# A two-block transformer kernel: another order of the opening stage, a norm's sum of squares by products with ones, and stores moved to ScalarE and GpSimd

## The chip, the cores and the metric

The kernel runs on one core of a Trainium2 chip. The metric is the device time of one execution in microseconds. The core has TensorE (PE, matrix products; PEld its weight loads), VectorE (DVE), ScalarE (ACT), GpSimd (POOL) and SyncE (SP); each works through its own queue in order, and waits on semaphores for the others and for transfers. SyncE computes nothing: it issues DMA transfers. ScalarE and GpSimd can issue them too, from their own queues, between their other instructions.

## What is computed

Two transformer blocks in a row on one sequence of 512 tokens with 1024 channels: the first with two layers (modulation from a condition vector, pooling, neighbourhood attention, retention, a convolutional feed-forward part), the second with latent attention, a long convolution (Hyena), attention to a memory of 256 tokens and a mixture of experts. Three pieces matter here, since they do not depend on the first block's result and are computed at the very start: the convolution filters, keys and values of the memory, and the first layer's modulation.

```python
def _hyena_filters(L, w1, b1, freq, w2, b2, w3, b3, decay):
    ...
    h = jnp.sin(fr[0] * (z @ w1.astype(f32) + b1.astype(f32)))
    h = jnp.sin(fr[1] * (h @ w2.astype(f32) + b2.astype(f32)))
    h = h @ w3.astype(f32) + b3.astype(f32)
    h = h * jnp.exp(-t01[:, None] * jnp.abs(decay.astype(f32))[None, :])
    ...
    return jnp.fft.rfft(k, axis=0)

def _mem_xattn(hx, hm, w_mq, w_mkv, w_mo):
    ...
    k, v = jnp.split(hm @ w_mkv, 2, axis=-1)
    ...

# in second_block, hm is _rms(mem, mem_norm_g[l]); in first_block:
mx = jnp.split(silu_c @ w_mod[l] + b_mod[l], 6, axis=-1)
```

## The kernel before

Activations lie with channels on the 128 partitions and tokens along the free dimension. A product of full precision is made of three (`mm3`, lines 198 to 200): each operand is split into a high part in the fast format and a low part, and high x high, low x high and high x low are summed in one bank of PSUM. A weight of 128x1024 is loaded by SyncE, its high part is cast by ScalarE (L181) and its low part subtracted by VectorE (L182). Products whose operands are plain f32 (L296, L309, L407, L1142, L1168) show up in the trace as two instructions each.

The opening is `first` (line 1666). It has five generators, each of which yields after a piece of work, and a written-out order of letters, `START` (line 53), and a shorter one, `SECOND`, say which generator goes on next. A framework below then puts the instructions of each engine in their final order, by its own estimate of when their inputs are ready; so the letters set priorities, and the order shown further down is what each engine's queue really holds.

- `f`: the filters (`hyena_filters`, line 1122). Small tables are loaded, two small products (L1142) each feed a sine: five VectorE operations bring the argument into range, ScalarE takes the sine (L1144 to L1120). Then, for each of two filter sets, eight products with `hy_w3` (L1168) whose results VectorE and ScalarE window and split, and a Fourier transform by products with tables (`transform`, L198 to L200 with `hs0h` and so on, 512 columns). Each transform pair is copied (`hodd`, L1193), added and subtracted by VectorE (L1194, L1195) into `ho`, which has one buffer, and stored to `kf_dram` (L1196); a row of alternating sums goes to `kx_dram`.
- `m`: the memory (`memory`, line 1436). Squares by ScalarE (L319, L322), their running sum by GpSimd (L323); a product with ones turns the sum over channels into a column per token (L296), a root and a reciprocal of a few columns follow, a product spreads it over the partitions again (L309), VectorE multiplies (L335) and each chunk is split into `mmh` (L343, ScalarE) and `mml` (L344, VectorE). Then eight key columns of 24 products each (256 wide), copied by ScalarE (L1450) and stored to `mk_dram`, and the values, 96 products of 512 columns in four PSUM banks, copied into `mvo`, which has one buffer, and stored to `mv_dram`.
- `d`: modulation (`modulation`, line 397). Sixteen weight tiles of 512 KB through two buffers, `mraw`, each used by two products of two rows (L407). These occupy a 32-column quarter of TensorE each. The other two thirds of the layer's modulation use the same code later, in the background.
- `h`: the eight loads of the stream. `n`: the norm of the tokens, behind which layer 0's first products (`lin<-ah`) wait.

Of the kernel before, what the change touches and what calls it, by code (L numbers as in the profile page):

```python
# [11 lines left out]
F32 = mybir.dt.float32  # L12
FR = mybir.dt.float32r
I32 = mybir.dt.int32
AF = mybir.ActivationFunctionType
ALU = mybir.AluOpType
AX = mybir.AxisListType

P = 128
D = 1024  # L20
KC = D // P
S = 512
C = 256
# [26 lines left out]
CONV = "a a a * b a b * * a a a b * a b a * b c c b b b * c b c * d d c c * c d * c d c d d d d d + +".split()  # L50


START = "m f m m m f f f m m f m f m m h h h h h h d f h f d d d d h f d d f d f d d m m m f d m n f f f d d n m m d d n m m d d n m n".split()
SECOND = "f n n n n f f n f n n f n".split()
TILES = 48

# [49 lines left out]
class Builder:  # L106
# [1015 lines left out]
    def hyena_filters(self):  # L1122

        nc, a = self.nc, self.a
        self.kf = self.tc.dram_tile([2, 2, P, 4, S], F32, name="kf_dram")
        self.kx = self.tc.dram_tile([2, 1, 3, S], F32, name="kx_dram")
        small = self.t([64, 6], F32, "hyv", 1)  # L1130
        nc.sync.dma_start(small, a["hyv"])
        zt = self.t([33, S], F32, "hz", 1)
        nc.sync.dma_start(zt, a["hyz"])
        w12 = self.t([64, 128], F32, "hw", 1)
        nc.sync.dma_start(w12[:33, :64], a["hy_w1"])
        nc.sync.dma_start(w12[:, 64:], a["hy_w2"])
        tcol = self.t([P, 16], F32, "htc", 1)
        nc.sync.dma_start(tcol, a["hytc"])
        x = zt
        for i in range(2):  # L1140
            ps = self.psum("pt")[:64, :]
            nc.tensor.matmul(ps, w12[:33 if i == 0 else 64, 64 * i:64 * i + 64], x, start=True, stop=True)  # L1142
            arg = self.t([P, S], F32, "he0", 1)[:64]
            nc.vector.tensor_scalar(out=arg, in0=ps, scalar1=small[:, 2 * i:2 * i + 1],  # L1144
                                    scalar2=small[:, 2 * i + 1:2 * i + 2], op0=ALU.add, op1=ALU.mult)
            y = self.t([65, S], F32, f"hh{i}", 1)
            self.sin(y[:64], arg)
            x = y[:64]
            yield
        nc.gpsimd.memset(y[64:65], 1.0)  # L1150
        skip = self.t([1, 2 * S], F32, "hskip", 1)
        nc.sync.dma_start(skip, a["hy_skip"])
        alt = self.t([P, 8], FR, "halt", 1)
        nc.vector.tensor_copy(alt, tcol[:, 8:16])
        for n in range(2):
            n0 = slice(1024 * n, 1024 * n + 1024)
            w3 = self.t([65, 1024], F32, "hw3", 1)
            nc.sync.dma_start(w3, a["hy_w3b"][:, n0])
            dec = self.t([P, 1024], F32, "hdec", 1)
            nc.sync.dma_start(dec, a["hy_decay"][:, n0].broadcast_to([P, 1024]))  # L1160
            nc.scalar.activation(out=dec, in_=dec, func=AF.Abs)
            both = [[[self.t([P, S], FR, f"hs{sd}" + x, 4) for _ in range(4)] for x in "hl"] for sd in range(2)]
            for tcn in range(4):
                h = []
                for d in range(2):
                    c = slice(512 * d, 512 * d + 512)
                    ps = self.psum("pt")
                    nc.tensor.matmul(ps, y[:, tcn * P:tcn * P + P], w3[:, c], start=True, stop=True)  # L1168
                    e = self.t([P, S], F32, f"he{d}", 1)
                    nc.scalar.activation(out=e, in_=dec[:, c], func=AF.Exp, scale=tcol[:, tcn:tcn + 1])  # L1170
                    nc.vector.tensor_tensor(out=e, in0=e, in1=ps, op=ALU.mult)
                    h.append(e)
                x = self.t([P, S], F32, "hx", 1)

                nc.vector.scalar_tensor_tensor(out=x, in0=h[1], scalar=tcol[:, 4 + tcn:5 + tcn], in1=h[0],
                                               op0=ALU.mult, op1=ALU.add)
                if tcn == 0:

                    nc.vector.tensor_tensor(out=x[:1], in0=x[:1], in1=skip[:, S * n:S * n + S], op=ALU.add)
                self.split(both[0][0][tcn], both[0][1][tcn], x)  # L1180
                x = self.t([P, S], F32, "hx", 1)
                nc.vector.tensor_tensor(out=x, in0=h[0], in1=h[1], op=ALU.subtract)
                self.split(both[1][0][tcn], both[1][1][tcn], x)
                yield
            for f in range(2):
                w = self.exact(a["dftk"][f])
                for im in range(2):
                    eo = [self.psum(("lin", "sc")[im]) for _ in range(2)]
                    for odd in range(2):
                        self.transform(eo[odd], w, 2 * im + odd, [x[2 * odd:2 * odd + 2] for x in both[im]])  # L1190
                    o = self.t([P, 2, S], F32, "ho", 1)
                    x = self.t([P, S], F32, "hodd", 1)
                    nc.scalar.copy(x, eo[1])  # L1193
                    nc.vector.tensor_tensor(out=o[:, 0], in0=eo[0], in1=x, op=ALU.add)  # L1194
                    nc.vector.tensor_tensor(out=o[:, 1], in0=eo[0], in1=x, op=ALU.subtract)  # L1195
                    nc.sync.dma_start(self.kf[n, f, :, 2 * im:2 * im + 2], o)  # L1196
                    yield
            ps = self.psum("pt")
            for i in range(8):
                odd, j, part = i // 4, i // 2 % 2, i % 2  # L1200
                nc.tensor.matmul(ps[:4], alt[:, 4 * odd:4 * odd + 4], both[odd][part][2 * odd + j], start=i == 0,
                                 stop=i == 7)
            o = self.t([P, 2, S], F32, "ho", 1)
            nc.scalar.copy(o[:4, 0], ps[:4])
            nc.sync.dma_start(self.kx[n].rearrange("o r s -> (o r) s"), o[:3, 0])
            yield

    def transform(self, ps, w, part, x):
# [227 lines left out]
    def memory(self):  # L1436

        nc, a = self.nc, self.a
        m = [self.t([P, 4, C], F32, "mm", 2) for _ in range(2)]
        for i in range(2):  # L1440
            nc.sync.dma_start(m[i], a["mT"][i])
        m = [m[k // 4][:, k % 4] for k in range(KC)]
        mh, ml = ([self.t([P, C], FR, "mm" + x, 8) for _ in range(KC)] for x in "hl")
        self.norm(m, (0, C), lambda k: self.col("mem_norm_g_2", k), None, mh, ml)
        yield
        self.mk = self.tc.dram_tile([KC, P, C], F32, name="mk_dram")
        for j in range(KC):
            ps = self.linear(self.weight(a["w_mk"][j], 1024), mh, ml, (0, C))
            x = self.t([P, C], F32, "mo", 2)
            nc.scalar.copy(x, ps)  # L1450
            nc.sync.dma_start(self.mk[j], x)
            yield
        self.mv = self.tc.dram_tile([2, P, D], F32, name="mv_dram")
        acc = [self.psum(t) for t in ("lin", "lin", "sc", "sc")]
        for k in range(KC):
            wh, wl = self.weight(a["w_mv"][k], 1024)
            for j in range(2):
                c = slice(j * P, j * P + P)
                for i in range(2):
                    d = slice(512 * i, 512 * i + 512)  # L1460
                    self.mm3(acc[2 * j + i], mh[k][:, c], ml[k][:, c], wh[:, d], wl[:, d], k == 0, k == KC - 1)
            yield
        for j in range(2):
            x = self.t([P, D], F32, "mvo", 1)
            for i in range(2):
                nc.scalar.copy(x[:, 512 * i:512 * i + 512], acc[2 * j + i])
            nc.sync.dma_start(self.mv[j], x)
        yield

    def out_half(self, i, ch, x, ks, ps=None):  # L1470
# [195 lines left out]
    def first(self):  # L1666
# [19 lines left out]
        ah, al = self.next_acts = [], []  # L1686
        norm = [self.norm_steps(self.h, SL[s], *self.mod_scale(0, 1, s), ah, al) for s in range(2)]
        steps = {"m": memory, "f": filters, "d": mod, "h": self.load_stream(), "n": norm[0]}
        for t in START:
            next(steps[t], None)  # L1690
# [651 lines left out]
```

## Time and profile before

| | |
|---|---|
| median of 3 runs | 2652.45 us (2650.92 to 2658.2) |
| profiled execution, its own time | 2654.92 us |
| its span, first to last instruction | 2653.1 us |
| mean granted TensorE clock | 0.977 of full |
| TensorE busy | 2511.2 us (95%), 14286 instructions |
| TensorE weight loads | 2005.6 us (76%) |
| VectorE busy | 1711.6 us (65%) |
| ScalarE busy | 1171.2 us (44%) |
| GpSimd busy | 432.8 us (16%) |
| DMA, mean | 139 GB/s |

The profile is of one execution; times in its views count from the span's start. A product's busy time overlaps that of the next, so the pitch of products is read from a stretch in which TensorE is busy throughout, divided by their number. Waits are put down to what ended last. The granted clock is 1.00 at 2.4 GHz and 0.50 at 1.2 GHz; it has records from 23 us on, and stands at 1.00 in the views before that.

### The profile page before, as it was taken

The page shows a single profiled execution, that of the slowest core. Times are in us where ns is not written, and L with a number is a line of the kernel's source. Part 1 is how long each engine was busy: PE and PEld are TensorE (multiplying, and loading weights), DVE is VectorE, ACT ScalarE, POOL GpSimd, SP SyncE. Part 2 cuts the span into 40 slices and gives each one's busy share as a digit, 9 for nine tenths or more (in the row PEclk, how much of TensorE's full clock was granted, in tenths as well). Part 3 has the DMA queues.
Part 4 walks back from the last instruction along what each step waited for, and adds up shares of the span by engine and source line. Part 5 has one row for each costly group of instructions (what it writes and reads, how often), then busy time and mean ns, then how long its engine had stood idle before and what let it go on. Part 6 is the DMA issues. An engine that isn't in the chain of part 4 may idle for free. (4 is left out here: it accounts for less than half of the span.)

```text
span 2653.1 us, 37574 instructions
## 1 busy us (share of the span) xinstructions
PE 2511.2 (95%) x14286; PEld 2005.6 (76%) x14286; DVE 1711.6 (65%) x2932; ACT 1171.2 (44%) x1971; POOL 432.8 (16%) x448
## 2 busy tenths in 40 slices
PE   7999999999999999989899999999999879989996
PEld 5578776788888888878777988888888768755553
DVE  6657766656667666477777664556788986345554
ACT  6545465555313313355456642335666554301112
POOL 3041121030000000142311200002400540221100
PEclk9999999999999999999999999999999989989998
DMA  7732223342345352252112533233312642689970
GB/s 244 272 132 89 84 80 103 101 152 77 96 124 158 97 182 85 77 168 66 52 40 63 164 102 95 94 100 119 102 49 96 220 133 87 247 319 367 379 316 33
DMA packets 114048, 368.92 MB, mean 139 GB/s; under 512 B 17988, under 2 KB 29648, under 8 KB 101450
## 3 DMA queue, kind: packets, MB, share of 16 engines
q1 hardware_dynamic: 110554, 358.10, 39.8%
q0 software_dynamic: 3312, 8.40, 0.9%
q8 instruction: 114, 1.87, 0.3%
q14 instruction: 68, 0.56, 0.1%
HBM read 356.95 MB, written 13.68 MB: 140 GB/s over the span
## 5 line engine op out<-in xcount | busy, mean ns | idle before, releaser
L198 PE MATMUL lin<-ah,whi 128*128 128x512 f32 (+1 forms) x1504 | 557.2, 371 | 19.0 <-ACT qd L224 9.3
L200 PE MATMUL lin<-al,whi 128*128 128x512 f32 (+1 forms) x1504 | 548.7, 366 | 1.6 <-DVE al L344 1.1
L199 PE MATMUL lin<-ah,wlo 128*128 128x512 f32 (+1 forms) x1504 | 546.1, 364 | 2.8 <-DVE wlo L182 2.8
L181 ACT CAST whi<-wraw 128x1024 fp32r<-128x1024 f32 (+2 forms) x297 | 298.0, 1006 | 313.1 <-PE sc L200 174.4
L182 DVE TENSOR_TENSOR wlo<-wraw,whi 128x1024 fp32r<-128x1024 f32 (+2 forms) x297 | 362.7, 1223 | 85.3 <-ACT whi L181 83.6
L198 PEld LDWEIGHTS lin<-ah,whi 128*128 128x128 f32 x1504 | 287.5, 191 | 69.1 <-ACT qd L224 10.6
L200 PEld LDWEIGHTS lin<-al,whi 128*128 128x128 f32 x1504 | 286.5, 191 | 50.2 <-issue 2.7
L199 PEld LDWEIGHTS lin<-ah,wlo 128*128 128x128 f32 x1504 | 287.3, 191 | 40.7 <-DVE wlo L182 3.3
L323 POOL TENSOR_TENSOR sqacc<-sqacc,sq 128x256 f32<-128x256 f32 (+1 forms) x101 | 128.6, 1279 | 1083.3 <-ACT sq L322 1082.0
L198 PE MATMUL sc<-ah,whi 128*128 128x256 f32 (+1 forms) x696 | 219.6, 316 | 0.0
L199 PE MATMUL sc<-ah,wlo 128*128 128x256 f32 (+1 forms) x696 | 219.3, 315 | 0.0
L200 PE MATMUL sc<-al,whi 128*128 128x256 f32 (+1 forms) x696 | 218.7, 315 | 0.0
L198 PEld LDWEIGHTS sc<-ah,whi 128*128 128x128 f32 x696 | 132.7, 191 | 10.8 <-issue 0.9
L199 PEld LDWEIGHTS sc<-ah,wlo 128*128 128x128 f32 x696 | 132.6, 191 | 10.2 <-DVE wlo L182 0.4
L200 PEld LDWEIGHTS sc<-al,whi 128*128 128x128 f32 x696 | 132.4, 191 | 8.0
L887 DVE SCALAR_TENSOR_TENSOR fv<-lin,vec,fv 128x511 f32<-128x511 f32 x67 | 50.2, 749 | 117.3 <-ACT fv L886 117.3
L1920 PE MATMUL lin<-ew,ex 128*64 128x256 f32 x864 | 115.5, 384 | 0.1
L445 DVE CUSTOM_DVE_ANT_0 mraw<-mraw,crow 128x512 f32<-128x512 f32 x128 | 86.9, 689 | 33.3 <-DMA mraw<-in_w_mod_rows 32.0
L199 PE MATMUL lin<-mh,wlo 128*128 128x512 f32 (+1 forms) x292 | 105.3, 361 | 1.6 <-DVE wlo L182 1.4
L198 PE MATMUL lin<-mh,whi 128*128 128x512 f32 (+1 forms) x292 | 105.3, 361 | 0.0
L200 PE MATMUL lin<-ml,whi 128*128 128x512 f32 (+1 forms) x292 | 104.8, 359 | 0.0
L1920 PEld LDWEIGHTS lin<-ew,ex 128*64 128x64 f32 x864 | 65.2, 136 | 46.3 <-issue 18.3
(636 smaller groups left out, 5346.6 us busy)
## 6 DMA issues: line engine op xcount, KB each, us to landing
ew<-in_w_moe SPq DMA_DIRECT2D x81, 1024.0 KB, 10.8
wraw<-in_w_up SPq DMA_DIRECT2D x88, 512.0 KB, 3.5
wraw<-in_w_in SPq DMA_DIRECT2D x61, 512.0 KB, 3.6
mraw<-in_w_mod SPq DMA_DIRECT2D x48, 512.0 KB, 3.5
mraw<-in_w_mod_rows SPq DMA_DIRECT2D x96, 256.0 KB, 2.8
wraw<-in_w_down SPq DMA_DIRECT2D x48, 448.0 KB, 3.3
wraw<-in_w_out SPq DMA_DIRECT2D x32, 512.0 KB, 3.6
wraw<-in_w_down SPq DMA_DIRECT2D x16, 512.0 KB, 3.6
```

What stands on the lines that cost most here:

```text
L181: nc.scalar.copy(hi[:, :n], raw[:, :n])
L182: nc.vector.tensor_tensor(out=lo[:, :n], in0=raw[:, :n], in1=hi[:, :n], op=ALU.subtract)
L198: mm(out, wh, xh, start=start, stop=False)
L199: mm(out, wl, xh, start=False, stop=False)
L200: mm(out, wh, xl, start=False, stop=stop)
L323: nc.gpsimd.tensor_tensor(out=acc, in0=acc, in1=sq, op=ALU.add)
L445: self.tc.keep_in_program_order(nc.vector.tensor_tensor_reduce(out=x, in0=raw, in1=self.crow[:, i, d], scale=1.0, scalar=0.0, op0=ALU.mult ...
L887: nc.vector.scalar_tensor_tensor(out=v[:, t0 + 1:t1], in0=ps[:, :t1 - t0 - 1], scalar=cw(0), in1=v[:, t0 + 1:t1], op0=ALU.mult, op1=ALU.add)
L1920: nc.tensor.matmul(ps[CAP * f:CAP * f + CAP, :256], xk, pieces(512 * k + 256 * f, 256), start=k == 0, stop=k == KC - 1, tile_position=(0, ...
```

## The change

`START` is another order, with the filters first and memory, modulation and stream mixed more finely. Memory's norm gets its sum over channels from eight products of the 128x128 ones matrix with the squares, summed in PSUM, so that the sum stands in all partitions at once; root and reciprocal are then 256 columns wide, and GpSimd multiplies the chunks. Squares come from ScalarE and VectorE in turn, in two buffers. The filters' five first loads, memory's eight key stores and the two `kx` stores are issued by ScalarE, the eight `kf` stores and the two `mv` stores by GpSimd.

```diff
--- before.py
+++ after.py
@@ -50,7 +50,7 @@
 CONV = "a a a * b a b * * a a a b * a b a * b c c b b b * c b c * d d c c * c d * c d c d d d d d + +".split()
 
 
-START = "m f m m m f f f m m f m f m m h h h h h h d f h f d d d d h f d d f d f d d m m m f d m n f f f d d n m m d d n m m d d n m n".split()
+START = "f m d d m f d d m f m d d m f m h m f h m d d m f h m h f d d h f h d f h d f d m h d m f m f d m n m f d n m f n m d n m n f".split()
 SECOND = "f n n n n f f n f n n f n".split()
 TILES = 48
 
@@ -1128,14 +1128,14 @@
         self.kf = self.tc.dram_tile([2, 2, P, 4, S], F32, name="kf_dram")
         self.kx = self.tc.dram_tile([2, 1, 3, S], F32, name="kx_dram")
         small = self.t([64, 6], F32, "hyv", 1)
-        nc.sync.dma_start(small, a["hyv"])
+        nc.scalar.dma_start(small, a["hyv"])
         zt = self.t([33, S], F32, "hz", 1)
-        nc.sync.dma_start(zt, a["hyz"])
+        nc.scalar.dma_start(zt, a["hyz"])
         w12 = self.t([64, 128], F32, "hw", 1)
-        nc.sync.dma_start(w12[:33, :64], a["hy_w1"])
-        nc.sync.dma_start(w12[:, 64:], a["hy_w2"])
+        nc.scalar.dma_start(w12[:33, :64], a["hy_w1"])
+        nc.scalar.dma_start(w12[:, 64:], a["hy_w2"])
         tcol = self.t([P, 16], F32, "htc", 1)
-        nc.sync.dma_start(tcol, a["hytc"])
+        nc.scalar.dma_start(tcol, a["hytc"])
         x = zt
         for i in range(2):
             ps = self.psum("pt")[:64, :]
@@ -1193,7 +1193,7 @@
                     nc.scalar.copy(x, eo[1])
                     nc.vector.tensor_tensor(out=o[:, 0], in0=eo[0], in1=x, op=ALU.add)
                     nc.vector.tensor_tensor(out=o[:, 1], in0=eo[0], in1=x, op=ALU.subtract)
-                    nc.sync.dma_start(self.kf[n, f, :, 2 * im:2 * im + 2], o)
+                    nc.gpsimd.dma_start(self.kf[n, f, :, 2 * im:2 * im + 2], o)
                     yield
             ps = self.psum("pt")
             for i in range(8):
@@ -1202,7 +1202,7 @@
                                  stop=i == 7)
             o = self.t([P, 2, S], F32, "ho", 1)
             nc.scalar.copy(o[:4, 0], ps[:4])
-            nc.sync.dma_start(self.kx[n].rearrange("o r s -> (o r) s"), o[:3, 0])
+            nc.scalar.dma_start(self.kx[n].rearrange("o r s -> (o r) s"), o[:3, 0])
             yield
 
     def transform(self, ps, w, part, x):
@@ -1441,14 +1441,28 @@
             nc.sync.dma_start(m[i], a["mT"][i])
         m = [m[k // 4][:, k % 4] for k in range(KC)]
         mh, ml = ([self.t([P, C], FR, "mm" + x, 8) for _ in range(KC)] for x in "hl")
-        self.norm(m, (0, C), lambda k: self.col("mem_norm_g_2", k), None, mh, ml)
+
+        ps = self.psum("pt")[:, :C]
+        for k in range(KC):
+            sq = self.t([P, C], F32, "mo", 2)
+            if k % 2:
+                nc.vector.tensor_tensor(out=sq, in0=m[k], in1=m[k], op=ALU.mult)
+            else:
+                nc.scalar.activation(out=sq, in_=m[k], func=AF.Square)
+            nc.tensor.matmul(ps, self.ones, sq, start=k == 0, stop=k == KC - 1)
+        r = self.t([P, C], F32, "mr", 1)
+        nc.scalar.activation(out=r, in_=ps, func=AF.Sqrt, scale=1.0 / D, bias=self.eps)
+        nc.vector.reciprocal(out=r, in_=r)
+        for k in range(KC):
+            nc.gpsimd.tensor_tensor(out=m[k], in0=m[k], in1=r, op=ALU.mult)
+            self.affine_split(mh[k], ml[k], m[k], self.col("mem_norm_g_2", k))
         yield
         self.mk = self.tc.dram_tile([KC, P, C], F32, name="mk_dram")
         for j in range(KC):
             ps = self.linear(self.weight(a["w_mk"][j], 1024), mh, ml, (0, C))
             x = self.t([P, C], F32, "mo", 2)
             nc.scalar.copy(x, ps)
-            nc.sync.dma_start(self.mk[j], x)
+            nc.scalar.dma_start(self.mk[j], x)
             yield
         self.mv = self.tc.dram_tile([2, P, D], F32, name="mv_dram")
         acc = [self.psum(t) for t in ("lin", "lin", "sc", "sc")]
@@ -1464,7 +1478,7 @@
             x = self.t([P, D], F32, "mvo", 1)
             for i in range(2):
                 nc.scalar.copy(x[:, 512 * i:512 * i + 512], acc[2 * j + i])
-            nc.sync.dma_start(self.mv[j], x)
+            nc.gpsimd.dma_start(self.mv[j], x)
         yield
 
     def out_half(self, i, ch, x, ks, ps=None):
```

What TensorE's queue holds at the very start, before (`sqacc` is the sum of squares, `tokw` its root, `mmh` and `mml` memory's split chunks):

```order
L296 MATMUL pt_152<-cmat,sqacc_129 128x1 x2
L309 MATMUL pt_158<-cmat,tokw_155 128x128 x2
L1142 MATMUL pt_206<-hz_199,hw_201 64x512
L198 MATMUL lin_226<-mmh_113,whi_221 128x256
L199 MATMUL lin_226<-mmh_113,wlo_222 128x256
L198 MATMUL lin_260<-mmh_113,whi_255 128x256
L199 MATMUL lin_260<-mmh_113,wlo_256 128x256
L200 MATMUL lin_226<-mml_121,whi_221 128x256
L198 MATMUL lin_226<-mmh_114,whi_221 128x256
```

The two steps of the norm, one filter product, then memory's first two columns side by side.

The same place after the change (`mo` are the squares, `pt_153` the bank of their sum, `bg` the modulation's):

```order
L1142 MATMUL pt_120<-hz_113,hw_115 64x512
L1452 MATMUL pt_153<-mo_154,cmat 128x256
L1452 MATMUL pt_153<-mo_157,cmat 128x256
L1452 MATMUL pt_153<-mo_160,cmat 128x256
L1452 MATMUL pt_153<-mo_163,cmat 128x256
L407 MATMUL bg_205<-mraw_206,csil 2x512
L1452 MATMUL pt_153<-mo_166,cmat 128x256
L1452 MATMUL pt_153<-mo_169,cmat 128x256
L407 MATMUL bg_205<-mraw_206,csil 2x512
L407 MATMUL bg_205<-mraw_210,csil 2x512 x2
L1452 MATMUL pt_153<-mo_172,cmat 128x256
L1452 MATMUL pt_153<-mo_175,cmat 128x256
```

and what follows it there:

```order
L1142 MATMUL pt_249<-hh_124,hw_115 64x512
L407 MATMUL bg_205<-mraw_262,csil 2x512 x2
L407 MATMUL bg_205<-mraw_266,csil 2x512 x2
L198 MATMUL lin_221<-mmh_137,whi_216 128x256
L198 MATMUL lin_276<-mmh_137,whi_271 128x256
L199 MATMUL lin_221<-mmh_137,wlo_217 128x256
```

The filter's first product stands first, the products with ones are mixed with modulation products, and the filter's second product and two more modulation tiles come ahead of memory's first column.

SyncE's queue where memory's key columns are computed, before (`hy` the stream, `mraw` modulation weights, `dftk` transform tables):

```order
L1706 DMA hy_88<-in_hT 128x768
L1451 DMA mk_dram<-mo_251 128x256
L180 DMA wraw_536<-in_w_mk 128x1024
L1451 DMA mk_dram<-mo_285 128x256
L180 DMA wraw_570<-in_w_mk 128x1024
L1451 DMA mk_dram<-mo_319 128x256
L1706 DMA hy_89<-in_hT 128x768
L1706 DMA hy_90<-in_hT 128x768
L1706 DMA hy_91<-in_hT 128x768
L1451 DMA mk_dram<-mo_429 128x256
L404 DMA mraw_611<-in_w_mod 128x1024
L1451 DMA mk_dram<-mo_463 128x256
```

and after:

```order
L180 DMA wraw_391<-in_w_mk 128x1024
L180 DMA wraw_443<-in_w_mk 128x1024
L1720 DMA hy_86<-in_hT 128x768
L180 DMA wraw_478<-in_w_mk 128x1024
L1720 DMA hy_87<-in_hT 128x768
L180 DMA wraw_531<-in_w_mk 128x1024
L404 DMA mraw_565<-in_w_mod 128x1024
L404 DMA mraw_569<-in_w_mod 128x1024
L180 DMA wraw_573<-in_w_mk 128x1024
L1720 DMA hy_88<-in_hT 128x768
```

The stores are gone from it; loads follow loads.

GpSimd's queue behind the last sum of squares of the opening, after the change (before, `px` stood directly behind that sum):

```order
L323 TENSOR_TENSOR sqacc_1288<-sqacc_1288,sq_1308 128x256
L1481 DMA mv_dram<-mvo_1032 128x1024
L1196 DMA kf_dram<-ho_672 128x1024
L1481 DMA mv_dram<-mvo_1036 128x1024
L1196 DMA kf_dram<-ho_701 128x1024
L1196 DMA kf_dram<-ho_734 128x1024
L1196 DMA kf_dram<-ho_759 128x1024
L1196 DMA kf_dram<-ho_1115 128x1024
L1196 DMA kf_dram<-ho_1155 128x1024
L1196 DMA kf_dram<-ho_1183 128x1024
L1196 DMA kf_dram<-ho_1208 128x1024
L818 MEMSET px_1284 128x16
```

The first store of memory's values stands ahead of the first filter store, and the pooling stage's `px` behind all of them.

## Rows read from the trace of the kernel before

**Rows 1.** Stretches of the opening: busy time of each engine, granted clock, DMA.

```profile
0.00:20.00 20.00, 5.50 (x16) 3.51 (x17) 6.21 (x13) 10.49 (x20) 6.79 (x14) 1.00 0.90 292
20.00:40.00 20.00, 18.96 (x135) 17.35 (x133) 17.87 (x26) 14.85 (x25) 5.68 (x4) 1.00 0.64 220
40.00:60.00 20.00, 16.68 (x67) 11.71 (x67) 13.20 (x16) 12.86 (x20) 7.33 (x6) 0.74 0.65 220
60.00:141.00 81.00, 79.28 (x318) 45.52 (x317) 53.24 (x76) 47.73 (x73) 5.66 (x9) 0.98 0.78 271
```

**Rows 2.** TensorE's waits from 0 to 200 us: total, times, longest.

```profile
PE bg L407 <- DMA mraw<-in_w_mod: 3.9, 2, 3.7
...
PE pt L309 <- DVE tokw L285: 1.3, 2, 0.7
```

**Rows 3.** Four stretches by TensorE's rate, columns as in group 1.

```profile
32.00:39.00 7.00, 7.00 (x60) 7.00 (x61) 6.90 (x6) 5.17 (x11) 4.68 (x4) 1.00 0.87 290
133.00:137.00 4.00, 4.00 (x19) 3.23 (x18) 3.64 (x7) 3.95 (x7) 0.00 (x0) 1.00 0.77 257
44.00:54.00 10.00, 10.00 (x28) 6.39 (x27) 5.15 (x6) 6.18 (x10) 2.56 (x2) 0.50 0.46 160
129.00:132.00 3.00, 3.00 (x11) 2.42 (x11) 2.58 (x5) 2.58 (x4) 0.00 (x0) 0.51 0.66 259
```

**Rows 4.** Timeline of TensorE: start, us, operation, idle time before.

```profile
12.18 1.01 PE L296 MATMUL pt<-cmat,sqacc 128*128 128x1 f32 x4 [12.18 <-POOL sqacc L323]
...
14.90 1.97 PE L1142 MATMUL pt<-hz,hw 33*64 33x512 f32 x2
...
18.64 0.58 PE L198 MATMUL lin<-mmh,whi 128*128 128x256 f32 x1 [1.77 <-ACT mmh L343]
...
30.87 1.07 PE L1142 MATMUL pt<-hh,hw 64*64 64x512 f32 x2 [0.32 <-ACT hh L1120]
...
43.32 3.39 PE L1168 MATMUL pt<-hw,hh 65*128 65x512 f32 x4 [3.85 <-ACT hh L1120]
...
60.06 1.03 PE L407 MATMUL bg<-mraw,csil 128*2 128x512 f32 x4
```

**Rows 5.** Timeline of ScalarE.

```profile
11.93 1.28 ACT L284 ACT_TABLE_LOAD   x1
...
26.33 0.37 ACT L1450 COPY mo<-lin 128x256 f32<-128x256 f32 x1 [1.69 <-PE lin L200]
```

**Rows 6.** Timeline of SyncE's queue and of VectorE: the last small filter load.

```profile
4.73 0.59 SPq L1138 DMA_DIRECT2D htc<-in_hytc  x1
...
8.54 0.40 DVE L1154 CAST halt<-htc 128x8 fp32r<-128x8 f32 x1 [7.67 <-DMA htc<-in_hytc]
```

**Rows 7.** VectorE: one row of its timeline, two groups of 0 to 60 us.

```profile
21.89 0.68 DVE L1118 SCALAR_TENSOR_TENSOR he<-he,he 64x512 f32<-64x512 f32 x1
...
L182 DVE TENSOR_TENSOR wlo<-wraw,whi 128x1024 fp32r<-128x1024 f32 x8 | 9.8, 1223 | 3.9 <-ACT whi L181 3.9
...
L344 DVE SCALAR_TENSOR_TENSOR mml<-nx,vec,mmh 128x256 fp32r<-128x256 f32 x8 | 3.5, 477 | 0.0
```

**Rows 8.** VectorE's reciprocals by form, whole span: busy us, mean ns.

```profile
L285 DVE RECIPROCAL tokw<-tokw 128x4 f32<-128x4 f32 x11 | 1.9, 173 | 6.9 <-ACT tokw L284 6.9
...
L285 DVE RECIPROCAL tokw<-tokw 128x8 f32<-128x8 f32 x6 | 1.2, 200 | 10.7 <-ACT tokw L284 10.7
```

**Rows 9.** GpSimd's L323 at 256 columns: 0 to 60 us, then whole span.

```profile
L323 POOL TENSOR_TENSOR sqacc<-sqacc,sq 128x256 f32<-128x256 f32 x9 | 6.9, 762 | 4.8 <-ACT sq L322 4.3
...
L323 POOL TENSOR_TENSOR sqacc<-sqacc,sq 128x256 f32<-128x256 f32 x70 | 78.8, 1133 | 412.9 <-ACT sq L322 411.8
```

**Rows 10.** DMA issues: queue, count, KB each, median us from issue to landing.

```profile
mraw<-in_w_mod SPq DMA_DIRECT2D x48, 512.0 KB, 3.5
...
kf_dram<-ho SPq DMA_DIRECT2D x8, 512.0 KB, 4.9
...
t_dram<-xrow POOLq DMA_DIRECT2D x4, 256.0 KB, 7.8
```

## The prediction

> **What bounds the kernel now.** I read the page's line of engine shares first: TensorE is busy nearly all the span, so an edit counts by what it does to TensorE's waits, to the rate of its products, and to how many it has. Then the table of stretches [rows 1]. In the first 20 us TensorE works 5.50 us, in the next two stretches 18.96 and 16.68: it stands idle 14.50 + 1.04 + 3.32 = 18.9 us before 60 us, and only 1.7 us in the 81 us after that. The opening's waits lie at its start; the rest of it is TensorE's own work.
>
> The timeline of TensorE says which they are [rows 4]: 12.18 us at the start for GpSimd's running sum of squares, and 3.85 us in the filters' first L1168 product for a sine from ScalarE. The waits by releaser add two [rows 2]: up to 0.7 us at a time in L309, and 3.9 us for the modulation's weights, 3.7 of them in one wait, which lies past the opening, at 179 us in the timeline. Two stretches have TensorE at half rate [rows 3]: from 44 to 54 us the granted clock is 0.50 (1.2 GHz), right behind the 3.85 us wait, and from 129 to 132 us it is 0.51, right behind the one in L309. Against 2.4 GHz the first loses some 5 us, the second 1.5. A product of 256 columns takes 7.00/60 = 0.12 us at the full clock, one of 512 about 4.00/19 = 0.21 [rows 3].
>
> **The first 30 us.** Before: the sum is handed over at 12.18 us and memory's first product starts at 18.64 [rows 4]; its first two columns are done by 26.33 [rows 5]. After: the filters' small inputs are ScalarE's first instructions. The last of them, issued at 4.73, was used at 8.54 [rows 6], 3.8 us on; issued from ScalarE some 3 us sooner, they let the first L1142 product start at 5.5 us. It takes 2.0 us [rows 4]. Eight products with ones follow, 256 columns wide in plain f32: half of an L1168 product, that is 3.39/4 = 0.85 us each at the low rate [rows 4], 6.8 us together; I charge the low rate, since TensorE comes from idleness. Between them stand two groups of modulation products (L407). A group costs 1.03 us [rows 4] at the full clock, up to twice that at the low one; I take 1.4. The sum is ready at 5.5 + 2.0 + 6.8 + 2.8 = 17 us.
>
> Behind it: VectorE first has an L1144 that waits for the second L1142 product (1.07 us [rows 4], and 0.7 as L1118 [rows 7]), then the reciprocal over 256 columns. No row shows that; it grows from 173 ns at 4 columns to 200 at 8 [rows 8], 6.7 ns a column, so an estimate of 0.2 + 248 x 0.0067 = 1.9 us and, as the lower bound, the 0.2 us of the small ones. The square root's table load of 1.28 us [rows 5] fits in while TensorE still sums. Then GpSimd multiplies, 256 columns a time. Its nearest operation, the L323 sum, took 762 ns in the first 60 us and 1133 over the kernel [rows 9]; I take 1.13 us, because VectorE's low halves run beside it. ScalarE's high half adds 0.5, as VectorE's low half L344 [rows 7]. First product: 17 + 1.8 + 1.9 + 1.1 + 0.5 = 22.3 us, 3.7 later than before. The other seven chunks come every 1.13 us, so the last is complete at 30.7, and the second column, 24 products of 0.12 us, ends at 33.6: **7.3 us later** than 26.33.
>
> The Trainium skill (SBUF — State Buffer, Who interferes with whom) says that a VectorE operation with two SBUF inputs and a GpSimd operation that reads SBUF shut each other out. By that rule each multiplication would queue behind an L344 of 0.48 us, 10 us for the eight instead of my 9; the trace agrees so far, as the 1133 ns stand against 762 for the same form.
>
> What TensorE has done meanwhile that it had to do later before: three groups of L407 (3.1) and the second L1142 product (1.0): -4.1.
>
> **The wait for the sine.** The second filter product ran at 30.87 before and its sine was ready at 43.3 [rows 4]. Now it runs at 18, and the rest of the chain starts when VectorE is through with the low halves at 30.7: six operations of at most 0.68 us and one weight split of 1.22 [rows 7], some 4.5 us, then a table load [rows 5] and the sine, ready at about 37. TensorE reaches L1168 at 33.6 + 22 x 0.12 + 1.0 = 37.2. The wait goes, **-3.9**, and with it the slow stretch, **-5.0**. But TensorE, starved until 30 us, will begin the rest at the low clock, as it did from 18.64 to about 23 us before: +2.3. What is late next is VectorE, which from 30 to 60 us carries the chain, the splits and the filters' taps; I leave it uncharged, its share from 40 us on was 66% [rows 1].
>
> **Fewer groups.** Where two to four modulation products stand side by side in TensorE's order, they run at once, and a group costs 1.03 us whatever its length. The order has 45 groups for layer 0 before and 42 now: -3.1. Ahead of layer 0's first product stand 23 now and 15 before, so eight come forward. The removed L296 and L309 pairs of memory are in the start times above.
>
> **The L309 wait** at 128 us has three transform products and one group put between its two halves: -0.7, and -1.5 for the slow stretch.
>
> **Loads.** SyncE loses 20 stores and five loads. Loads stood queued behind those stores; but TensorE waited only 3.9 us for any load to 200 us [rows 2], and 3.7 of it at 179 us, where I expect the same again, since two weight buffers still have to turn round before a group of seven. So freeing SyncE is worth about nothing. The price side: the order asks for twelve modulation tiles where the transforms run, with two buffers, and a load lands 3.5 us after issue [rows 10]. I charge +2.5; between 0 and 5.
>
> The Trainium skill (DMA: Bandwidth & Descriptors, Issuing engines are not separate DMA queues) says that spreading DMAs over engines saves only their issue time. By that rule the moved stores alone give nothing, as above; no run here shows it yet.
>
> **Stores.** The filters' output has one buffer: each store must land before VectorE may write the next, 1.4 us for its two operations (two like L1118 [rows 7]). A store took 4.9 us to land from SyncE; rows stored from GpSimd took 7.8 [rows 10]. From the first store to layer 0's first product TensorE now has about 39 us of its own work (84 transform products, 8 groups, 6 of L1168 at 0.9, half of the low-clock price, small ones), and five stores must land in that time: the chain shows when 5 x (landing + 1.4) passes 39, at a landing of 6.4 us. I take 4.9 and 0.3 for GpSimd's issue, so nothing; at 7.8 it costs 7, with the next store 11.
>
> **Sum**: +7.3 - 4.1 - 3.9 - 5.0 + 2.3 - 3.1 - 2.2 + 2.5 = -6.2 us. Behind the opening the work and its order stay, so the gain goes through to the end. The profiled execution took 2654.92 us, 2.5 above the median of 2652.45; 2654.9 - 6.2 = 2648.7, against the median 2646.2. I say **2646**.
>
> **Rivals.** About 0.3%, 8 us, is what a measurement of this kernel can tell from no change.
>
> Slower: the GpSimd stores. If they land in 7.8 us or more, TensorE waits 11 us before and in layer 0's first products, and one such wait brings another slow stretch like that at 44 us, 5 more: -6.2 + 16 = +10, 2662. For it: GpSimd's row of 7.8, and memory's value store, also single-buffered, standing ahead of the first filter store in GpSimd's queue. Against: that row's stores were issued four at a time beside weight loads. It decides from 6.4 us on. Chance 0.14.
>
> Faster by more: the opening packs better than I charge. GpSimd at 0.76 us a multiplication (-2.6), no waits on modulation tiles (-2.5), the clock up before 17 us (-3) and no second slow start (-2.3): -6.2 - 10.4 = -16.6, 2636. For it: after 60 us the old order ran 81 us with 1.7 us of waiting, so an order of this kind hides what it plans for. Chance 0.38, taken from a gain of 8 on.
>
> No effect: what is won early is lost to the loads. DMA is busy 0.78 of the time from 60 to 141 us [rows 1], and 5 MB of modulation weights come forward into that stretch; then the gain ends at 0 to 2 us, 2651. Chance 0.05.
>
> The forecast itself, a gain under 8 us: 0.43. So faster 0.39, same 0.47, slower 0.14. Range: 2636 from the good case, 2660 from within the store case.
>
> **What would show it.** Right: first TensorE product near 5.5 us; memory's first product near 22, paced by GpSimd; no long wait in L1168 and no half clock at 44 us; layer 0's first product near 146 us, which is 141 and the eight groups, less the gain so far. Wrong: waits of VectorE's L1194 for the kf store over 3 us; TensorE waiting for mraw again and again between 95 and 145 us; a reciprocal far from 1.9 us.

## The result, and the profile after

The changed kernel takes 2669.2 us (median of 5 runs, 2668.26 to 2671.78) against 2652.45 before: 1.006 times as long, 95% interval 1.0045 to 1.0075, some 16 us **slower** where a gain of 6 was forecast. The profiled execution took 2668.26 us, 13.3 more than that of before. On the page TensorE is as busy as it was (2511.2 us before); the span is longer:

```profile
span 2666.5 us, 37578 instructions
...
PE 2511.0 (94%) x14294; PEld 1999.1 (75%) x14294; DVE 1704.3 (64%) x2928; ACT 1172.7 (44%) x1968; POOL 440.2 (17%) x459
```

The stretches of the opening in the changed kernel, columns as in [rows 1]; the fourth ends where layer 0's first product starts:

```profile
0.00:20.00 20.00, 11.44 (x32) 4.22 (x32) 8.56 (x16) 7.52 (x12) 2.09 (x8) 1.00 0.75 254
20.00:40.00 20.00, 17.41 (x90) 11.04 (x91) 12.06 (x20) 14.08 (x21) 7.16 (x8) 1.00 0.83 293
40.00:60.00 20.00, 19.85 (x139) 16.20 (x138) 19.14 (x22) 15.72 (x26) 5.76 (x3) 1.00 0.85 281
60.00:163.70 103.70, 89.39 (x339) 47.55 (x338) 49.59 (x73) 55.25 (x84) 15.79 (x19) 0.93 0.71 241
120.00:125.00 5.00, 4.54 (x11) 3.05 (x11) 2.86 (x5) 2.15 (x3) 0.54 (x1) 0.66 0.55 221
135.00:145.00 10.00, 9.56 (x34) 6.10 (x31) 3.08 (x9) 5.20 (x8) 0.00 (x0) 0.53 0.49 158
...
60.00:105.00 45.00, 37.95 (x146) 19.48 (x145) 17.36 (x19) 22.69 (x36) 11.24 (x11) 1.00 0.81 279
110.14:163.69 53.55, 46.29 (x171) 24.84 (x170) 30.94 (x52) 29.48 (x45) 3.77 (x7) 0.87 0.61 205
```

Up to 60 us TensorE works 48.7 us where it worked 41.1 [rows 1]: the start of the new order is better. Then it stands idle 103.7 - 89.4 = 14.3 us, against 1.7 in the 81 us of [rows 1], half of it up to 105 us (45.0 - 37.95 = 7.1) and half behind that. The granted clock is 0.93 there where it was 0.98; it is 0.66 in the 5 us from 120 and 0.53 in the 10 us from 135 us on. The last two rows are used further down. TensorE's timeline of the changed kernel (start, us, operation, idle time before) shows where its stages begin:

```profile
6.41 1.94 PE L1142 MATMUL pt<-hz,hw 33*64 33x512 f32 x2 [6.41 <-DMA hw<-in_hy_w]
8.28 3.44 PE L1452 MATMUL pt<-mo,cmat 128*128 128x256 f32 x8
...
21.74 0.50 PE L198 MATMUL lin<-mmh,whi 128*128 128x256 f32 x2 [0.63 <-ACT mmh L343]
...
36.40 1.88 PE L1168 MATMUL pt<-hw,hh 65*128 65x512 f32 x4
...
60.04 0.79 PE L198 MATMUL lin<-whi,mmh 128*128 128x512 f32 x1
...
76.28 0.50 PE L198 MATMUL lin<-whi,mmh 128*128 128x512 f32 x1 [2.02 <-ACT whi L181]
...
104.92 0.40 PE L198 MATMUL lin<-hs0h,whi 128*128 128x512 f32 x1
...
120.45 0.79 PE L198 MATMUL sc<-hs1h,whi 128*128 128x512 f32 x1 [3.21 <-DVE ho L1195]
...
133.00 2.96 PE L407 MATMUL bg<-mraw,csil 128*2 128x512 f32 x8 [1.57 <-DMA mraw<-in_w_mod]
...
163.69 0.40 PE L198 MATMUL lin<-ah,whi 128*128 128x512 f32 x1
```

Memory's values start at 60.04 us, and 95 of their 96 products run before the first transform product at 104.92. Before, filter set 1's transforms came first (61.0 us), then the values (86.9), then set 2's transforms (up to 141.0), and layer 0's first product at 141.07. Now it comes at 163.69, 22.6 us later; nine more rows of L407 in the timeline stand ahead of it (24 against 15), some 1.03 us each that need no doing later. From there to the end the changed kernel takes 9.2 us less (2502.8 against 2512.0), and 22.6 - 9.2 = 13.4 is the whole difference of the two spans.

That the transforms' data were there long before is shown by the tile `hs0h`, set 1's split taps: L1201's small products read it from 65.2 us on, the transforms from 104.9.

```profile
L198 PE MATMUL lin<-hs0h,whi x16: 392/396/796, 104.9 to 157.9; 128*128 128x512 f32 x16
...
L1201 PE MATMUL pt<-hs0h,halt x4: 387/397/792, 65.2 to 148.8; 128*4 128x512 f32 x4
```

What held them is in the code: `lin` and `sc` have two PSUM banks each, `memory` takes all four with its tenth `m` (`acc`) and gives them back behind the 96th product, and a transform pair takes two. In the old letters the seventh `f` (set 1's first transforms) stands ahead of the tenth `m`, in the new ones behind it.

The hold takes more than the banks. Set 1's two transform tables are cast (L193) at 56.6 and 63.0 us, and then lie in two of the three `whi` buffers (L181 and L193 share them) until the transforms read them from 104.9 us on. The values' weights have the third one alone: the last five of their casts (81.9 to 101.2 us) each start within 0.1 us of the end of a product with the weight before, and TensorE waits 3.8 us for `whi` (L198) in three waits. ScalarE's timeline of the changed kernel:

```profile
56.60 1.05 ACT L193 CAST whi<-wraw 128x1024 fp32r<-128x1024 f32 x1
...
63.01 1.04 ACT L193 CAST whi<-wraw 128x1024 fp32r<-128x1024 f32 x1
...
92.39 1.04 ACT L181 CAST whi<-wraw 128x1024 fp32r<-128x1024 f32 x1 [5.18 <-PE sc L199]
```

With the transforms in one block, the next thing they wait for is `ho`. VectorE's and GpSimd's timelines: the adds end at 109.83, the store goes out at 110.14, and VectorE may write again at 119.11.

```profile
17.75 1.73 DVE L1455 RECIPROCAL mr<-mr 128x256 f32<-128x256 f32 x1
...
109.15 0.68 DVE L1195 TENSOR_TENSOR ho<-lin,hodd 128x512 f32<-128x512 f32 x1
...
119.11 0.69 DVE L1194 TENSOR_TENSOR ho<-sc,hodd 128x512 f32<-128x512 f32 x1 [5.77 <-DMA kf_dram<-ho]
```

```profile
19.63 7.53 POOL L1457 TENSOR_TENSOR mm<-mm,mr 128x256 f32<-128x256 f32 x8 [17.33 <-DVE mr L1455]
...
110.14 0.56 POOL L1196 DMA_DIRECT2D kf_dram<-ho x1 [3.82 <-DVE ho L1195]
```

The tile `ho` to 260 us, changed kernel: who waited, and the stores' landing.

```profile
DMA kf_dram<-ho: 13.7, 3
...
PE sc L198: 3.5, 2
...
DMA to landing us min/median/max: 2.9/3.5/9.1
```

### The profile page after: what moved, and what is told of

Its sections match the earlier page's. It is cut to its first block, busy times and chain, and to the rows that moved or that the text cites. A ratio compares the mean times of both kernels' runs of the same rounds, so it can differ in the third digit from the quotient of the medians.

```text
span 2666.5 us, 37578 instructions
## 1 busy us (share of the span) xinstructions
PE 2511.0 (94%) x14294; PEld 1999.1 (75%) x14294; DVE 1704.3 (64%) x2928; ACT 1172.7 (44%) x1968; POOL 440.2 (17%) x459
## 5 line engine op out<-in xcount | busy, mean ns | idle before, releaser
L198 PE MATMUL lin<-ah,whi 128*128 128x512 f32 (+1 forms) x1504 | 554.9, 369 | 16.7 <-ACT qd L224 10.6
L181 ACT CAST whi<-wraw 128x1024 fp32r<-128x1024 f32 (+2 forms) x297 | 297.4, 1004 | 312.5 <-PE sc L200 164.9
L198 PEld LDWEIGHTS lin<-ah,whi 128*128 128x128 f32 x1504 | 286.5, 191 | 64.6 <-ACT qd L224 12.8
L323 POOL TENSOR_TENSOR sqacc<-sqacc,sq 128x256 f32<-128x256 f32 (+1 forms) x94 | 123.2, 1316 | 1074.2 <-ACT sq L322 1073.4
L198 PE MATMUL sc<-ah,whi 128*128 128x256 f32 (+1 forms) x696 | 220.2, 317 | 0.0
L198 PEld LDWEIGHTS sc<-ah,whi 128*128 128x128 f32 x696 | 133.0, 191 | 10.3 <-ACT ah L268 0.2
L198 PE MATMUL lin<-mh,whi 128*128 128x512 f32 (+1 forms) x292 | 105.3, 360 | 0.0
L1934 PEld LDWEIGHTS lin<-ew,ex 128*64 128x64 f32 x864 | 65.2, 136 | 46.3 <-issue 18.3
```

Of the source, the lines that this page charges most:

```text
L181: nc.scalar.copy(hi[:, :n], raw[:, :n])
L198: mm(out, wh, xh, start=start, stop=False)
L323: nc.gpsimd.tensor_tensor(out=acc, in0=acc, in1=sq, op=ALU.add)
L1934: nc.tensor.matmul(ps[CAP * f:CAP * f + CAP, :256], xk, pieces(512 * k + 256 * f, 256), start=k == 0, stop=k == KC - 1, tile_position=(0, ...
```

## The experiments

Ratios are against the kernel before, run on the same chip, with 95% intervals; 0.001 is 2.65 us. The changed kernel's is 1.0060.

**Round 1: which part of the change.** The letters alone, and the change without each of its parts.

```diff
# e1_start_only: before.py          # e1_old_start: after.py with the old START
-START = "m f m m m f f f m m ..."
+START = "f m d d m f d d m f ..."
# e1_all_sp: after.py               # e1_stores_only: before.py with the four reverse edits
-nc.gpsimd.dma_start(self.kf[n, f, ...], o)
+nc.sync.dma_start(self.kf[n, f, ...], o)
-nc.scalar.dma_start(self.kx[n]..., o[:3, 0])
+nc.sync.dma_start(self.kx[n]..., o[:3, 0])
-nc.scalar.dma_start(self.mk[j], x)
+nc.sync.dma_start(self.mk[j], x)
-nc.gpsimd.dma_start(self.mv[j], x)
+nc.sync.dma_start(self.mv[j], x)
```

> The kernel before with nothing changed but the letters of START. Theory A (the order: all values of memory now stand ahead of the transforms, so weights for them and eight more groups of modulation weights are loaded in one stretch, 60 to 105 us, and the two filter sets then have nothing left beside them, 105 to 164 us): the whole loss comes with the letters, 2662 to 2670 us. Theory B (the stores: kf_dram's stores from GpSimd land up to 9 us after issue, VectorE's L1194 waits for them, and TensorE behind it): the letters alone lose at most 3 us, 2646 to 2655 us.

Measured 1.0051 (1.0034 to 1.0067), 2669.2 us: the letters alone cost as much as the whole change. Set 1's first transform product comes at 111.37 us, as theory A has it.

> The changed kernel with the old letters of START; the new sum of squares and the moved stores stay. Theory A: the loss is gone, 2645 to 2655 us. Theory B: the stores still land late beside the old order, 2658 to 2668 us.

Measured 1.0010 (1.0001 to 1.0018), 2657.2 us, between the two ranges and nearer to theory A's: nearly all of the loss is gone.

> The changed kernel with its four kinds of stores back on SyncE; letters, sum of squares and ScalarE's early loads stay. Theory A: no gain, within 3 us of the changed kernel or slower, since loads now stand behind stores again: 2666 to 2675 us. Theory B: VectorE's waits in L1194 go, with the half clock behind them: 2652 to 2660 us.

Measured 1.0070 (1.0057 to 1.0083), 2672.0 us: the loss stays with every store on SyncE, so GpSimd's queue is not its cause. TensorE waits only 0.8 us for `ho` there.

> The kernel before with its four kinds of stores moved to ScalarE and GpSimd, as in the change, and nothing else. Theory A: within 3 us of the kernel before, 2649 to 2656 us. Theory B: slower by 6 to 14 us, 2658 to 2666 us.

Measured 1.0019 (1.0010 to 1.0028), 2660.3 us: the time lies in theory B's range, the difference of 5.6 us from this chip's runs of before (2654.6) between the theories. Beside the old letters the moved stores cost some 5 us.

**Round 2: banks or loads, and the norm.**

```diff
# e2_set1_first: after.py, one m moved (the tenth, from behind the sixth f)
-... f h m h f d d h f h d f h d f d m h d m f ...
+... f h h f d d h f h d f h d f d m m h d m f ...
# e2_before_values_first: before.py, the tenth m moved the other way
-... h d f h f d d d d h f d d f d f d d m m m f ...
+... h d m f h f d d d d h f d d f d f d d m m f ...
# e2_half_loads: after.py, w_mk and w_mv
-nc.sync.dma_start(raw[:, :n], src)
+nc.sync.dma_start(raw[:, :512], src[:, :512])   (its splits read raw[:, :512] twice)
# e2_norm_only: after.py with the old START and the four stores on SyncE
```

> The changed kernel with one letter of START moved: the tenth m (memory's first value step, which takes the four lin and sc banks for all 96 value products) stands behind the tenth f instead of ahead of the seventh, so filter set 1's 48 transform products run ahead of the values as before. Banks theory (the values hold the banks, all 96 transforms queue behind them and the two filter sets lose the work that stood between them): 8 to 17 us come back, 2652 to 2661 us. Loads theory (weights and modulation tiles brought forward keep the transfers full from 60 to 105 us): most of the loss stays, as 22 modulation tiles still stand ahead of layer 0 against 28 and 16: 2662 to 2670 us.

Measured 1.0028 (1.0017 to 1.0038), 2659.3 us: one letter gives back 8.5 us. TensorE's timeline of this run: the transforms start at 62.06 us, and one wait for `ho` is left, as the values' first product takes a bank that set 1's last pair still holds.

```profile
62.06 0.80 PE L198 MATMUL lin<-hs0h,whi 128*128 128x512 f32 x1
...
91.11 0.50 PE L198 MATMUL lin<-whi,mmh 128*128 128x512 f32 x1 [3.71 <-DVE ho L1195]
...
147.20 0.40 PE L198 MATMUL lin<-ah,whi 128*128 128x512 f32 x1
```

> The inverse: the kernel before with its tenth m moved ahead of the seventh f, so that the values take the banks before filter set 1's transforms. Banks theory: slower than before by 6 to 15 us, 2660 to 2670 us. Loads theory: the letters of modulation and loads are the old ones, so less than 4 us: 2650 to 2658 us.

Measured 1.0099 (1.0084 to 1.0114), 2677.0 us: the same letter costs the old order 26 us, more than either theory gave it. The first transform product waits for the copy that frees the values' bank:

```profile
114.17 0.50 PE L198 MATMUL lin<-hs0h,whi 128*128 128x512 f32 x1 [0.29 <-ACT mvo L1466]
```

> The changed kernel with its 16 memory weights (keys and values) loaded only in their first 512 columns, which are used twice: 4.2 MB less to load in the opening, the products and splits as many as before. Banks theory: at most 4 us gained, 2665 to 2670 us. Loads theory: 8 to 14 us gained, 2655 to 2661 us.

This run uses the first 512 columns of the memory's weights in place of the last 512 too. Measured 1.0047 (1.0034 to 1.0060), 2664.6 us: 3.4 us back for 4.2 MB less, which its interval and the changed kernel's (1.0045 to 1.0075) do not part. Loads are at most a small part; with fewer of them TensorE's waits for `whi` go, but layer 0's first product still comes at 161.6 us.

> The kernel before with the new sum of squares and ScalarE's early loads of the filters' tables; the letters and the stores are the old ones. By the difference between the stores moved alone (+5.6 us) and the stores moved with the new sum (+2.6 us), the new sum is worth about -3 us: 2649 to 2654 us. If its price of +7.3 us in the first 30 us had come through, 2656 to 2662 us.

Measured 1.0029 (1.0020 to 1.0038), 2658.6 us. The number is that of the second theory, the way is not: memory's last key product ends at 56.1 us, earlier than the 60.1 of before, and yet layer 0's first product comes at 148.3, 7.3 us later than before. Four more L407 rows (19 against 15) stand ahead of it; the rest is lost behind the keys. In 60 to 148.3 us TensorE stands idle 88.3 - 83.7 = 4.6 us, at a clock of 0.96:

```profile
60.00:148.30 88.30, 83.68 (x321) 46.35 (x320) 53.40 (x77) 47.50 (x74) 5.40 (x10) 0.96 0.71 240
```

**Round 3: the one buffer.**

```diff
# e3_two_ho: after.py   # e3_set1_first_two_ho: e2_set1_first   # e3_before_two_ho: before.py
-o = self.t([P, 2, S], F32, "ho", 1)       (both places)
+o = self.t([P, 2, S], F32, "ho", 2)
-zt = self.t([33, S], F32, "hz", 1)
+zt = self.t([P, S], F32, "hodd", 1)[:33]
-w12 = self.t([64, 128], F32, "hw", 1)
+w12 = self.t([P, S], F32, "hx", 1)[:64, :128]
# e3_set1_letters: before.py with e2_set1_first's START
```

The two lower edits make room: two small tables move into buffers that are used only later.

> The changed kernel with two buffers for ho, the filters' output, so that VectorE's L1194 need not wait for the store before last to land (the tiles hz and hw lie in the later hodd and hx, to make room). If the single buffer with its store is a large part of the loss behind the values: TensorE's 3.5 us for ho and the half clock behind it (1.7 us) go, and more of the 13.7 us that VectorE waits there: 5 to 10 us gained against the changed kernel, 2659 to 2664 us. If the loss is the order alone: within 3 us, 2666 to 2671 us.

Measured 1.0042 (1.0029 to 1.0056), 2662.0 us: 4.8 us back, just under the 5 to 10 that were expected, and the two intervals overlap. No product waits for `ho` any more, but from 60 us to layer 0's first product TensorE still stands idle 98.4 - 87.2 = 11.2 us, 7.2 of them up to 105 us, beside the values, and the clock still falls to half behind them:

```profile
60.00:158.40 98.40, 87.18 (x326) 47.53 (x325) 46.83 (x69) 54.02 (x82) 15.76 (x19) 0.91 0.73 253
```

> The run e2_set1_first (tenth m behind the tenth f) with two buffers for ho. There the values' first product waited 3.7 us at 91 us for the last pair's ho, and the clock fell to half behind it (some 1.7 us). With the store as the cause both go: 5 us under e2_set1_first, +1 to +4 us against the kernel before. With another cause: as e2_set1_first, +6 to +9.

Measured 0.9982 (0.9973 to 0.9991), 2646.3 us: **faster than both kernels**, 13 us under e2_set1_first where 5 were expected. The clock stays up from 60 us to layer 0's first product, which comes at 139.2:

```profile
60.00:139.20 79.20, 76.15 (x316) 45.63 (x316) 50.36 (x73) 54.69 (x83) 16.61 (x19) 1.00 0.78 282
```

> The kernel before with the new letters of START, but the tenth m behind the tenth f; sum of squares and stores as before. Banks theory: the letters cost nothing but by that one letter, so within 3 us of the kernel before, -3 to +3. If the rest of the letters (modulation tiles early, stream loads spread) cost by themselves: +5 to +12.

Measured 1.0006 (0.9997 to 1.0015), 2653.1 us: without the one letter, the letters cost nothing that can be told.

> The kernel before with two buffers for ho and nothing else. VectorE waits only 3.5 us for the stores there and TensorE next to nothing for ho: within 2 us of the kernel before by every theory; a gain of over 3 would show that the buffer held up the old order too.

Measured 1.0016 (1.0006 to 1.0025), 2655.6 us: 4 us slower, a miss. Beside the old letters the second buffer gains nothing; why it costs 4 us was not tried.

**Round 4: the hold on the banks by itself, and the other parts in the best order.**

```diff
# e4_other_banks: after.py          # e4_other_banks_two_ho: e3_two_ho
-eo = [self.psum(("lin", "sc")[im]) for _ in range(2)]
+eo = [self.psum("pt") for _ in range(2)]
# e4_set1_two_ho_old_norm: e3_set1_letters with e3's two buffers
# e4_norm_on_vector: e3_set1_first_two_ho
-nc.gpsimd.tensor_tensor(out=m[k], in0=m[k], in1=r, op=ALU.mult)
+nc.vector.tensor_tensor(out=m[k], in0=m[k], in1=r, op=ALU.mult)
```

> The changed kernel, letters and all, but the filters' transforms take their two PSUM banks under the tag pt instead of lin and sc, which the memory's values hold. If the hold on the banks is the cause: filter set 1's products run from about 62 us beside the values, layer 0's first product comes at or before 148 us, and 8 to 17 us come back: 2652 to 2661 us. If the cause is the order of the letters or the loads alone, 2664 to 2670 us; if the two pt banks, which other products of the filters use too, become the new wait, in between.

Measured 1.0025 (1.0014 to 1.0036), 2659.5 us: 9.3 us back with the letters untouched. The tile `hs0h` in this run: the transforms are read into `pt` from 65.4 us on, beside the values, which start at 61.31.

```profile
L198 PE MATMUL pt<-hs0h,whi x16: 392/398/801, 65.4 to 149.5; 128*128 128x512 f32 x16
```

> As e4_other_banks, with two buffers for ho. If hold and single buffer are two separate waits: another 3 to 7 us under e4_other_banks. If the pt banks limit the transforms now: within 3 us of it.

Measured 0.9987 (0.9979 to 0.9996), 2650.3 us: another 10 us, where 3 to 7 were expected. The hold on the banks and the single buffer are two waits, and without both the changed kernel's own letters beat the kernel before.

> The best run so far (e3_set1_first_two_ho, -5 us against the kernel before) without the new sum of squares, the moved stores and ScalarE's early loads. If sum and stores cost time by themselves, as beside the old letters: faster than that run by 3 to 8 us, -8 to -13 us against the kernel before. If their worth hangs on the order around them: within 3 us of it, or slower by up to 6, since memory's first product then waits for GpSimd's sum again.

Measured 1.0017 (1.0008 to 1.0026), 2658.0 us: 9 us slower than with the new sum, the moved stores and ScalarE's early loads. Their worth hangs on what is around them, by more than was allowed for, and not on the order alone: with the same letters and one buffer these parts cost 5.8 us (e3_set1_letters 1.0006, e2_set1_first 1.0028), with two they save 9. The second buffer, too, brings nothing here: 1.0017 against the 1.0006 of e3_set1_letters, 2.9 us slower, with intervals that overlap.

> The best run so far (e3_set1_first_two_ho) with the sum's eight multiplications by the reciprocal on VectorE instead of GpSimd. If GpSimd's pace (7.53 us for the eight in the changed kernel) sets when memory's first columns end: 2 to 4 us gained. If TensorE's start at 20 to 30 us is hidden again further on, or VectorE is as slow since it makes the low halves too: within 2 us.

Measured 1.0000 (0.9991 to 1.0009), 2653.4 us: 4.8 us slower than e3_set1_first_two_ho (the intervals touch at 0.9991), another miss. A multiplication takes VectorE 413 ns where it takes GpSimd 974, and the first memory product comes 0.9 us earlier, at 22.1 us; it is lost again behind that.

## Why the prediction was wrong, step by step

**The first 30 us: right.** First product 6.41 us (5.5 expected), memory's first product 21.74 (22.3), the reciprocal 1.73 us (1.9). GpSimd's eight multiplications took 7.53 us, 0.94 each against the 1.13 that was taken. Memory's second column ended at 32.7 us (33.6 expected); before it ended at 26.65, and 26.33 was the copy of the first, so the 7.3 us came to 6.1. The Trainium skill (SBUF — State Buffer, Who interferes with whom) has VectorE's two-input operations shut out GpSimd's reads. The trace agrees in kind: L344 took 567 ns on average beside GpSimd's multiplications in e3_set1_first_two_ho and 473 without them in e4_norm_on_vector; but that is 0.1 us a chunk, and the 10 us that the rule was read to give did not come.

**Sine and slow stretch: right.** L1168 starts at 36.40 us without a wait and the clock is 1.00 from 40 to 60 us; the new start at half rate, charged with 2.3, shows in no window. By 60 us seven rows of L407 are done that had not begun before, 7.2 us: more than the -3.4 of the terms up to there.

**Stores: the step that failed.** "TensorE now has about 39 us of its own work" from the first store to layer 0's first product, so that stores landing below 6.4 us would cost nothing. The prediction had the order right, with nearly all the transforms behind the values (84 of 96 in its 39 us), but it put the waits inside these two blocks at nothing, but for the 2.5 of the loads: that an order which waited 1.7 us in 81 would again hide what it plans for was assumed, not read. Its 0.21 us a product of 512 columns is low too: the 19 counted in 4.00 us include some that lie partly outside, and the starts are 0.23 apart, 2 us more for the 84. Those 39 us took 163.7 - 110.1 = 53.6, with the eight groups that were counted and a median landing of 3.5 us: TensorE stood idle 7.3 of them, and the mean clock of 0.87 is worth 7.0. Another 7.1 us it stood idle beside the values, from 60 to 105. Against before, from 60 us on, TensorE's idle time grew by 14.3 - 1.7 = 12.6; a mean clock of 0.93 over 103.7 us against 0.98 over 81 is worth 7.3 - 1.6 = 5.7; the rest of the 22.6 are two more L407 rows (2.1) and 2.2 that no view assigns. What stood in the place of the overlap is the hold on the banks: with it taken away, letters untouched, 9.3 us came back, and with the second buffer 10 more.

**The slower rival: right sign, wrong cause.** It made the loss hang on GpSimd's landing, with 7.8 us as its mark. Its sign was seen, a wait of VectorE's L1194 of 5.77 us: landing was 3.5 us at the median, and the one of 9.1 cost the 3.21 us wait of TensorE and the half clock from 120 us. But with every store on SyncE TensorE waited 0.8 us for `ho`, and the loss was 1.0070. So the single buffer is where one of the waits shows, not what decides; that is the order, which leaves the transforms in one block with little beside them. The Trainium skill (DMA: Bandwidth & Descriptors, Issuing engines are not separate DMA queues) gives spreading DMAs over engines the issue time alone. Beside the new letters the runs agree (1.0060 and 1.0070, intervals overlapping); beside the old ones the moved stores cost 1.0019, with VectorE waiting 9.2 us for stores to land where it waited 3.5, and TensorE 2.2 us for `ho` where it waited none. Whether the queue does that, or the framework's order around it, no run shows.

**Loads.** Charged 2.5; TensorE's waits for modulation tiles, behind transfers, came to 5.0 us to 200 us. Those for `whi`, 3.8 us, stand behind three casts, two of which waited for the weight buffer: they are gone in e2_set1_first and e4_other_banks, where the tables are read at once, but also in e2_half_loads, so that loads have a part in them. 4.2 MB less brought 3.4 us back, within the intervals. The term was low by a few us at most, not by the error.

**What is shown, and what is not.** The banks are shown from three sides: the tenth `m` moved behind set 1's transforms (-8.5 us), the same letter moved ahead of them in the old kernel (+26), and other banks with no letter moved (-9.3). The second buffer was tried in five pairs. With the new sum and the stores on GpSimd it brought -4.8 (intervals overlap), -12 and -10 us; with the old sum and the stores on SyncE +4 beside the old letters and +2.9 (intervals overlap) in the very order in which it brought -12. So it is a second wait beside the hold only together with the new sum and the moved stores; which of the two makes it one is open, as no run has two buffers with the one and not the other. The Trainium skill (Perfetto Trace Analysis, Matmuls) asks that independent matmul groups rotate through different PSUM banks so that one's evacuation overlaps the next; here other banks let more than the evacuation overlap: in e4_other_banks the two groups' products run side by side from 65.4 us on, and 9.3 us come back. Open is why the sum of squares alone costs 7.5 us beside the old letters, and the stores alone 5, where both together cost 2.6. With the sum alone, the transforms start earlier and yet end later, with several waits under 1.5 us between; which of the framework's moves does it was not tried.

## What to carry to other kernels

When a written-out order is changed, ask of every step that moves what it takes and how long it keeps it: a step that holds all banks of a tag puts everything that needs that tag behind itself, however early its letters stand, and what is loaded for that work keeps its buffers meanwhile. A stage that was hidden is hidden by the work between its pieces; put the pieces in one block, and its waits show, with the slower clock behind them: 39 us of work took 53.6 here. And a part's cost measured in one place can turn into a gain in another: with the same letters the sum and the stores cost 5.8 us with one output buffer and saved 9 with two.

## What was not expected of the hardware

Stores of the same 512 KB from the same queue landed in 2.9 to 9.1 us, where the eight from SyncE before took 4.2 to 6.2; the slowest went out at 110.14 us, ahead of memory's second value store and among four weight and modulation loads issued between 106.22 and 111 us; from 110.1 to 120.5 the DMA engines were busy 0.98 of the time. In the changed kernel the half clock (0.50, 1.2 GHz) came each time behind waits: from 120.5 to 123 us behind one of 3.21 us, from 135 to 144 behind one of 1.57 and short ones.
